# Triangular inverses of a hybrid encoder: from 32x32 elimination on two engines to 16x16 elimination with TensorE products

## The chip, the cores and the metric

The kernel runs on one core of a Trainium2 chip. A core has a matrix engine (TensorE, PE in the profile, with its weight loads as PEld), VectorE (DVE), ScalarE (ACT), GpSimd (POOL), and a queue of DMA transfers that SyncE (SP) issues. Each engine works through its own list of instructions in order and waits for the others by semaphores. The metric is the device time in microseconds from start to end of one execution; it is measured several times, and the median is given.

## What is computed

A bidirectional encoder of two layers on 512 tokens and 1024 features. Each layer normalises its input, projects it once, and splits the columns among three mixers: windowed attention, a gated DeltaNet and an RWKV-7 mixer, the last two in both directions. Their outputs are joined, projected and added to the residual; then comes a gated feed-forward block. The part that matters here is this, from the DeltaNet:

```python
def gated_delta_chunked(q, k, v, g, beta):        # C = 64 tokens per chunk
    ...
    decay = jnp.exp(jnp.where(tril, gc[..., :, None] - gc[..., None, :], -jnp.inf))
    k_beta = k * beta[..., None]
    lower = jnp.where(strict, jnp.einsum('bhnid,bhnjd->bhnij', k_beta, k) * decay, 0.0)
    a_mat = lower + jnp.eye(C, dtype=lower.dtype)
    rhs = jnp.concatenate([v * beta[..., None], k_beta * jnp.exp(gc)[..., None]], -1)
    sol = lax.linalg.triangular_solve(a_mat, rhs, left_side=True, lower=True, unit_diagonal=True)
    ...

def rwkv7_scan(r, w, k, v, a, b):
    ...
    def step(state, inp):
        r_t, w_t, k_t, v_t, a_t, b_t = inp
        sa = jnp.einsum('bhvk,bhk->bhv', state, a_t)
        state = (state * w_t[:, :, None, :] + sa[..., None] * b_t[:, :, None, :]
                 + v_t[..., None] * k_t[:, :, None, :])
        return state, jnp.einsum('bhvk,bhk->bhv', state, r_t)
```

The DeltaNet solves one unit triangular 64x64 system per head, chunk and direction (6 heads, 8 chunks, 2 directions, per layer). The kernel computes RWKV-7 in chunks of 64 too, which gives the same kind of system (4 heads, 8 chunks, 2 directions). The kernel forms the inverse (I-N)^-1 of each of these systems, N strictly triangular, and the scans then multiply by it.

## The kernel before

Activations lie with features on the 128 partitions and the 512 tokens along the row. A projection is 24 matmuls of 128x512 (`product`, L319 to L321: eight k-tiles, each weight and each activation split in two parts). ACT and POOL make the split of the weights (L308, L309) as they arrive.

One layer goes through these stages: RWKV projections; the preparation of RWKV (`rwkv_prep`, for two pairs of heads) in turn with DeltaNet projections and their convolution (`dn_conv`); the RWKV inverses; the RWKV scan of eight steps, with attention projections beside it; `dn_prep`, which forms the DeltaNet matrices; `rwkv_out`; the DeltaNet inverses, with five blocks of attention (`attn_head`) beside them; the DeltaNet scan with the gate projections and more attention; the output projection; the feed-forward block.

A 64x64 matrix lies as `tile[:, chunk, 0:64]`, two heads above each other on the partitions, so a 128-row tile of eight chunks has 32 diagonal 32x32 blocks (four 32-row bands times eight chunks). The inverse of them is made in three steps.

1. Gather. For each band of 32 rows, one ACT copy of 32x256 puts the diagonal blocks of eight chunks into a tile `dpk` of 128 x 32 problems x 32 columns (L511 for RWKV, 16 per layer; L984 for the DeltaNet with the sign turned, 24 per layer; DeltaNet has 24 problems of each direction and 8 empty places).
2. `invert`. DVE transposes `dpk` so that each partition holds whole matrices (L383 or L385), 30 steps of forward elimination follow, each a product and a sum (L390, L391) on r x j columns, r + j = 31, the second waiting for the first; then two transposes (L397, L398) give the inverse as it lies and transposed. RWKV has one such chain, on DVE. The DeltaNet has two, the forward direction on DVE and the backward one on POOL, written in turn, with one block of attention after every sixth step.
3. `finish_inverse` fills in the 32x32 block off the diagonal of each 64x64 matrix by two small products per matrix (L411, a copy by ACT at L413, L417, a copy by ACT at L421) and ACT copies the diagonal blocks into place (L425, again a band of 32x256 at a time).

An attention block goes through PE (scores, L842), DVE (row maximum, L843), ACT (exponential, L852), DVE (L853 to L856), PE (transpose, L859), ACT (copy, L861), PE (L863).

The order on each engine is fixed when the kernel is built: a scheduler places instructions by priority as their inputs come, and tiles of a pool are handed out in the program's order, so a tile's new writer waits for the last reader of the old one. PSUM tiles have four pools: two for projections, three for RWKV and attention projections, two for the DeltaNet and attention, one for attention outputs.

The loop that both stages of the change touch is, for the DeltaNet:

```python
fw, bw = invert(dpks[0], True, V, work[:, :256]), invert(dpks[1], False, G, work[:, 256:])
for i in range(31):
    next(bw)
    next(fw)
    if i % 6 == 5:
        next(att, None)
inv = [run(fw), run(bw)]
```

## Time and profile before

| | |
|---|---|
| median of three runs | 1736.58 us (1732.81 to 1736.79) |
| span of the profiled execution, first to last instruction | 1732.2 us |
| PE busy | 1537.9 us, 89% |
| DVE, ACT, POOL busy | 952.5, 821.4, 704.9 us |
| mean granted clock of PE | 0.929 |

For the profiled execution only its span is known; the 4.4 us between the median and that span are taken as what lies around the span. The page gives totals by engine, and the groups of instructions by line. A table of stretches gives each engine's busy time between two points of the span, with the granted clock of PE as a share of full speed. A timeline gives single instructions, with the idle time ahead of each in brackets and the instruction whose end released it. Line numbers are those of the kernel before.

### The profile page before, as it was taken

To read this page: it belongs to the slowest core of one execution; us is meant where nothing else is said; L and a number is where in the kernel's file an instruction comes from. 1 tells how busy PE (TensorE), PEld (TensorE's weight loads), DVE (VectorE), ACT (ScalarE), POOL (GpSimd) and SP (SyncE) were. 2 spreads that over 40 slices of the span, in tenths; PEclk is the share of its full clock that TensorE was granted. 3 is DMA by queue.
4 is the path that set the end of the run, shared out by engine and by line. 5 is a ranking of instruction groups with operands and counts; after the bars stand their busy time and mean duration, and the time that the engine had idled before them with its cause. 6 is when DMAs were issued, how large, how long until landed. Compare 5 with 4: busy or idle time off the path is not lost. (4 is left out here: it accounts for less than half of the span.)

```text
span 1732.2 us, 29160 instructions
## 1 busy us (share of the span) xinstructions
PE 1537.9 (89%) x11500; PEld 1204.0 (70%) x11500; DVE 952.5 (55%) x1583; ACT 821.4 (47%) x1541; POOL 704.9 (41%) x632
## 2 busy tenths in 40 slices
PE   7988789359999999999998897982799999999997
PEld 4676666247678888888876676651577788888885
DVE  6478945775535555531136797578563455555001
ACT  5556453446445444443335754362744544444321
POOL 4321323431165555545543122426013655555553
PEclk9989979658999999999999998995799999999998
DMA  5311211100043333333342012220002333333332
GB/s 166 79 39 50 63 48 44 37 1 15 26 128 92 97 97 98 97 104 113 114 104 74 20 50 50 59 66 1 2 21 80 110 98 98 97 97 97 93 99 91
DMA packets 230537, 126.07 MB, mean 73 GB/s; under 512 B 23656, under 2 KB 221416, under 8 KB 230400
## 3 DMA queue, kind: packets, MB, share of 16 engines
q1 hardware_dynamic: 228624, 121.02, 25.0%
q10 hardware_dynamic: 1776, 3.20, 0.6%
q8 instruction: 90, 1.47, 0.4%
q14 instruction: 47, 0.39, 0.1%
HBM read 117.84 MB, written 6.34 MB: 72 GB/s over the span
## 5 line engine op out<-in xcount | busy, mean ns | idle before, releaser
L309 POOL TENSOR_TENSOR wl<-wr,wh 128x512 fp32r<-128x512 f32 (+1 forms) x408 | 555.9, 1365 | 760.9 <-ACT wh L308 714.5
L319 PE MATMUL ps<-hh,wh 128*128 128x512 f32 x1248 | 502.7, 403 | 21.2 <-ACT wh L308 18.6
L320 PE MATMUL ps<-hl,wh 128*128 128x512 f32 x1248 | 502.1, 402 | 0.0
L321 PE MATMUL ps<-hh,wl 128*128 128x512 f32 x1248 | 498.7, 400 | 0.4 <-POOL wl L309 0.4
L308 ACT ACTIVATE wh<-wr 128x512 fp32r<-128x512 f32 (+1 forms) x408 | 250.8, 618 | 444.5 <-PE ps L320 393.4
L319 PEld LDWEIGHTS ps<-hh,wh 128*128 128x128 f32 x1248 | 236.4, 190 | 80.2 <-ACT wh L308 19.5
L320 PEld LDWEIGHTS ps<-hl,wh 128*128 128x128 f32 x1248 | 236.3, 189 | 55.8 <-issue 3.7
L321 PEld LDWEIGHTS ps<-hh,wl 128*128 128x128 f32 x1248 | 235.8, 189 | 55.6 <-issue 3.9
L1063 DVE TENSOR_TENSOR p<-ps,p 128x512 f32<-128x512 f32 x16 | 11.1, 692 | 198.8 <-PE ps L321 198.8
L859 PE MATMUL ps<-cst,cv 128*128 128x128 f32 x120 | 24.9, 341 | 85.0 <-DVE cv L856 84.5
L320 PE MATMUL ps<-p,wh 128*128 128x512 f32 x256 | 99.6, 389 | 0.0
L319 PE MATMUL ps<-p,wh 128*128 128x512 f32 x256 | 99.6, 389 | 0.0
L321 PE MATMUL ps<-p,wl 128*128 128x512 f32 x256 | 99.6, 389 | 0.0
L1040 DVE TENSOR_TENSOR tr<-ps,rb 128x512 f32<-128x512 f32 x44 | 30.4, 692 | 100.3 <-PE ps L321 100.3
L859 PEld LDWEIGHTS ps<-cst,cv 128*128 128x128 f32 x120 | 15.7, 168 | 95.5 <-issue 67.4
L747 POOL TENSOR_TENSOR sm<-sm,gl 128x384 f32<-128x384 f32 x12 | 10.8, 903 | 129.9 <-DVE sm L776 72.8
L1043 DVE SCALAR_TENSOR_TENSOR td<-tr,par,td 128x511 f32<-128x511 f32 x44 | 39.1, 889 | 34.9 <-ACT td L1042 34.9
L1043 DVE SCALAR_TENSOR_TENSOR tr<-td,par,tr 128x511 f32<-128x511 f32 x44 | 36.5, 830 | 35.0 <-ACT tr L1042 35.0
L319 PEld LDWEIGHTS ps<-p,wh 128*128 128x128 f32 x256 | 48.1, 188 | 10.0
L321 PEld LDWEIGHTS ps<-p,wl 128*128 128x128 f32 x256 | 48.1, 188 | 9.9
L320 PEld LDWEIGHTS ps<-p,wh 128*128 128x128 f32 x256 | 48.1, 188 | 9.9
L279 POOL TENSOR_TENSOR tr<-tr,tr 128x512 f32<-128x512 f32 x32 | 42.8, 1337 | 28.0 <-issue 8.7
(292 smaller groups left out, 2597.6 us busy)
## 6 DMA issues: line engine op xcount, KB each, us to landing
wr<-ffn_w_up SPq DMA_DIRECT2D x176, 256.0 KB, 2.9
wr<-w_in SPq DMA_DIRECT2D x88, 256.0 KB, 2.8
wr<-ffn_w_down SPq DMA_DIRECT2D x80, 256.0 KB, 2.8
wr<-w_in SPq DMA_DIRECT2D x24, 128.0 KB, 2.4
p<-scr ACTq DMA_DIRECT2D x12, 256.0 KB, 3.6
wr<-w_out SPq DMA_DIRECT2D x32, 96.0 KB, 2.6
wr<-w_out SPq DMA_DIRECT2D x16, 192.0 KB, 3.0
p<-xt SPq DMA_DIRECT2D x8, 256.0 KB, 3.7
```

The source lines that it names most:

```text
L279: G.tensor_tensor(acc, self.acc, sq, add)
L308: S.activation(hi[:, :n, :], raw[:, :n, :], AF.Copy)
L309: G.tensor_tensor(lo[:, :n, :], raw[:, :n, :], hi[:, :n, :].bitcast(F32), sub)
L319: PE.matmul(o, wh, xh, start=k == 0, stop=False)
L320: PE.matmul(o, wh, xl, start=False, stop=False)
L321: PE.matmul(o, wl, xh, start=False, stop=k == n - 1)
L747: G.tensor_tensor(gs, state, flat(gl, step), mult)
L859: PE.transpose(pp[:, P * j : P * j + P], scs[g][:, P * j : P * j + P], ident)
L1040: V.tensor_tensor(u, o, nf.rb, mult)
L1043: V.scalar_tensor_tensor(a[:, 1:], u[:, :-1], w(0), a[:, 1:], mult, add)
L1063: V.tensor_tensor(x1[j], o, x1[j], add)
```

## The change

The elimination works on 16x16 blocks, and what the 32x32 inverse has beside them comes from products on PE. Both DeltaNet directions go through one chain of DVE instructions; POOL no longer eliminates. The ACT gathers by bands become one DVE instruction on all 128 rows with a mask (`diag32`: the left half times a 0/1 column plus the right half, of which the wrong parts are zero). In `invert`:

- L406 gathers the 16x16 diagonal halves of a `dpk` (128x512, masked), L411 transposes them (half as many columns as before); ACT keeps the part off the diagonal in `dpk` (L413), POOL clears the rest (L414).
- 14 steps of elimination, L421 and L422, on X x r x j columns with r + j = 15; X is 2 for RWKV and 4 for the DeltaNet (two halves, two directions).
- Per set of problems two transposes (L430, L431), three masked ACT copies (L434 to L436), and three groups of products with tiles of 32x32 and 16 columns, one product per problem and band: L440, an ACT copy (L442), L445, a DVE sum (L446), L449, a DVE sum (L450). A group has 128 products for RWKV and 96 for each DeltaNet direction.

In `finish_inverse` (L466 and L472 are the products that were L411 and L417) the copies of the diagonal blocks become one masked copy of 128 rows and two copies of 32 rows for eight chunks, where there were four of 32 rows. The DeltaNet loop has 16 turns with one block of attention after every third, five in all as before.

```diff
+    for name, half in (("m16", 16), ("m32", 32)):
+        first = (i // half % 2 == 0).astype(np.float32)
+        add(name, np.stack([first, 1 - first, -first, first - 1], 1))
...
-    def invert(dpk, upper, E, work):
-        L = p4(32, 32)
-        if upper:
-            V.transpose(L, dpk.rearrange("q p t -> q t p"))
-        else:
-            V.transpose(L.rearrange("p s t -> p t s"), dpk.rearrange("q p t -> q t p"))
-        yield
-        for j in range(1, 31):
-            r = 31 - j
-            tmp = work[:, : r * j].rearrange("p (r j) -> p r j", j=j)
-            E.tensor_tensor(tmp, L[:, j + 1 : 32, j : j + 1].broadcast_to([P, r, j]), L[:, j : j + 1, 0:j].broadcast_to([P, r, j]), mult)
-            E.tensor_tensor(L[:, j + 1 : 32, 0:j], L[:, j + 1 : 32, 0:j], tmp, add)
+    def diag32(dst, mt, upper):
+        lo, hi = mt[:, :, 0:32], mt[:, :, 32:64]
+        m = C("m32")
+        if upper:
+            V.scalar_tensor_tensor(dst, hi, m[:, 1:2], lo, mult, add)
         else:
+            V.scalar_tensor_tensor(dst, lo, m[:, 0:1], hi, mult, add)
+
+    def invert(st, dpks, uppers, sign, work, np_):
+        n = len(dpks)
+        m = C("m16")
+        s0 = 0 if sign > 0 else 2
+        L = p4(1024)
+        dc, o1c, o2c = p4(2, 32, 16), p4(2, 32, 16), p4(2, 32, 16)
+        halves = [(slice(0, 16), slice(16, 32)), (slice(16, 32), slice(0, 16))]
+        views = []
+        for x, (dpk, upper) in enumerate(zip(dpks, uppers)):
+            k = 1 if upper else 0
+            first, second = halves[0 if upper else 1]
+            V.scalar_tensor_tensor(dc[:, x], dpk[:, :, second], m[:, s0 + k : s0 + k + 1], dpk[:, :, first], mult, add if sign > 0 else sub)
...
+            V.transpose(byt, dc[:, x].rearrange("q p t -> q t p"))
+            S.activation(dpk[:, :, second], dpk[:, :, second], AF.Copy, scale=m[:, s0 + 1 - k : s0 + 2 - k])
+            G.memset(dpk[:, :, first], 0.0)
             yield
+        X = 2 * n
+        Lv = L[:, : 256 * X].rearrange("p (x r c) -> p x r c", r=16, c=16)
+        for j in range(1, 15):
+            r = 15 - j
+            tmp = work[:, : X * r * j].rearrange("p (x r j) -> p x r j", x=X, j=j)
+            V.tensor_tensor(tmp, Lv[:, :, j + 1 : 16, j : j + 1].broadcast_to([P, X, r, j]), Lv[:, :, j : j + 1, 0:j].broadcast_to([P, X, r, j]), mult)
+            V.tensor_tensor(Lv[:, :, j + 1 : 16, 0:j], Lv[:, :, j + 1 : 16, 0:j], tmp, add)
+            yield
...
+            V.transpose(o1c[:, x].rearrange("q p c -> q c p"), byt)
+            V.transpose(o2c[:, x].rearrange("q p c -> q c p"), bys)
+            o1, o2 = p4(32, 32), p4(32, 32)
+            u = slice(0, np_)
+            S.activation(o1[:, u, first], o1c[:, x, u], AF.Copy, scale=m[:, 1 - k : 2 - k])
+            S.activation(o1[:, u, second], o1c[:, x, u], AF.Copy, scale=m[:, k : k + 1])
+            S.activation(o2[:, u, second], o2c[:, x, u], AF.Copy, scale=m[:, k : k + 1])
+            pw = ps(st, (P, 32, 16))
+            blocks = [(p, slice(h, h + 32)) for p in range(np_) for h in range(0, P, 32)]
+            for p, hs in blocks:
+                PE.matmul(pw[hs, p, :], dpk[hs, p, :], o2c[hs, x, p, :], start=True, stop=True)
+            G.memset(dpk[:, :, second], 0.0)
+            S.activation(dpk[:, u, first], pw[:, u], AF.Copy)
+            px2 = ps(st, (P, 32, 16))
+            for p, hs in blocks:
+                PE.matmul(px2[hs, p, :], o1[hs, p, :], dpk[hs, p, first], start=True, stop=True)
+            V.scalar_tensor_tensor(o2[:, u, first], o2c[:, x, u], m[:, 1 - k : 2 - k], px2[:, u], mult, add)
+            px1 = ps(st, (P, 32, 16))
+            for p, hs in blocks:
+                PE.matmul(px1[hs, p, :], dpk[hs, p, :], o1c[hs, x, p, :], start=True, stop=True)
+            V.tensor_tensor(o1[:, u, second], px1[:, u], o1[:, u, second], add)
...
             for i in range(0, len(grp), 8):
-                mt = grp[i][1]
+                p, mt, _ = grp[i]
+                S.activation(mt[:, :, ra : ra + 32], o1[:, p : p + 8, :], AF.Copy, scale=m[:, ra // 32 : ra // 32 + 1])
                 for h in (0, 64):
+                    S.activation(mt[h + rb : h + rb + 32, :, rb : rb + 32], o1[h + rb : h + rb + 32, p : p + 8, :], AF.Copy)
...
-        for i in range(0, n, 8):
-            p, mt, _ = units[i]
-            for h in range(0, P, 32):
-                S.activation(mt[h : h + 32, :, h % 64 : h % 64 + 32], o1[h : h + 32, p : p + 8, :], AF.Copy)
...
-            for h in range(0, P, 32):
-                S.activation(st["dpk"][h : h + 32, 8 * u : 8 * u + 8, :], gb[h : h + 32, :, h % 64 : h % 64 + 32], AF.Copy)
+            diag32(st["dpk"][:, 8 * u : 8 * u + 8, :], gb[:, :, 0:64], True)
...
-        o1, o2 = run(invert(rw["dpk"], True, V, t2("r")))
+        ((o1, o2),) = run(invert("r", [rw["dpk"]], [True], 1.0, t2("r"), 32))
...
-        work = cv()
-        fw, bw = invert(dpks[0], True, V, work[:, :256]), invert(dpks[1], False, G, work[:, 256:])
-        for i in range(31):
+        bw = invert("d", dpks, [True, False], -1.0, cv(), 8 * NPAIR_DN)
+        for i in range(16):
             next(bw)
-            next(fw)
-            if i % 6 == 5:
+            if i % 3 == 2:
                 next(att, None)
-        inv = [run(fw), run(bw)]
+        inv = run(bw)
```

The scheduler then places the instructions anew. Lines L319 to L321 of before are L323 to L325 of the changed kernel, and the attention lines L842 to L863 are L895 to L916. In the rows below a name is a tile with its number: `ps` a PSUM tile, `p` one of the 20 tiles of four KB per partition, `hh`/`hl` and `wh`/`wl` the parts of activations and weights.

PE before, layer 0, where the RWKV inverse's first product stands: behind the last of a projection's 24 matmuls.

```order
L319 MATMUL ps_2258<-hh_147,wh_2267 128x512
L320 MATMUL ps_2258<-hl_148,wh_2267 128x512
L321 MATMUL ps_2258<-hh_147,wl_2268 128x512
L411 MATMUL ps_1629<-p_1626,p_631 32x32 x16
L411 MATMUL ps_1629<-p_1626,p_656 32x32 x16
L417 MATMUL ps_1665<-p_1625,tr_1630 32x32
L411 MATMUL ps_1702<-p_1626,p_1171 32x32 x16
L411 MATMUL ps_1702<-p_1626,p_1196 32x32 x5
L417 MATMUL ps_1665<-p_1625,tr_1630 32x32 x31
```

PE now, at the same stage: the products of the inverse stand inside a projection (`ps_2353`), and `L746` is a product of `dn_prep` that sums the squares of q or k (L693 before).

```order
L746 MATMUL ps_2218<-td_2216,cst 128x512
L323 MATMUL ps_2353<-hh_117,wh_2356 128x512
L324 MATMUL ps_2353<-hl_118,wh_2356 128x512
L325 MATMUL ps_2353<-hh_117,wl_2357 128x512
L323 MATMUL ps_2353<-hh_126,wh_2362 128x512
L440 MATMUL ps_1594<-p_1553,p_556 32x16 x128
L746 MATMUL ps_2224<-td_2222,cst 128x512
L445 MATMUL ps_1725<-p_556,p_1589 32x16 x128
L449 MATMUL ps_1855<-p_1552,p_556 32x16 x128
L466 MATMUL ps_1985<-p_1590,p_631 32x32 x16
```

Of that projection 14 matmuls stand ahead of L440. What follows the first L466 are the small products of `dn_prep` (L774 and L775); the rest of the projection and the whole next one have moved behind the inverse, among the products of the scan.

DVE before, end of the DeltaNet elimination of layer 0 (`den`, `nmx`, `es` belong to attention): block 4 ends, then the transposes with block 5 between them.

```order
L856 TENSOR_SCALAR cv_3127<-cv_3127,den_3141 128x256
L856 TENSOR_SCALAR cv_3128<-cv_3128,den_3141 128x256
L397 STREAM_TRANSPOSE p_3228<-p_2919 128x32x32
L843 ISA cv_3188,mx_3190<-ps_3191,cst,sink_86 128x256
L843 ISA mx_3190 128x1
L843 ISA cv_3189,mx_3190<-ps_3194,cst,sink_86 128x256
L843 ISA mx_3190 128x1
L398 STREAM_TRANSPOSE p_3229<-p_2919 128x32x32
L847 TENSOR_TENSOR es_3198<-sink_86,mx_3190 128x2
L848 TENSOR_SCALAR nmx_3197<-mx_3190 128x2
L397 STREAM_TRANSPOSE p_3233<-p_2917 128x32x32
L398 STREAM_TRANSPOSE p_3234<-p_2917 128x32x32
```

DVE now, at the same place: the end of block 4, then the transposes with block 5.

```order
L909 TENSOR_SCALAR cv_3397<-cv_3397,den_3411 128x256
L909 TENSOR_SCALAR cv_3398<-cv_3398,den_3411 128x256
L430 STREAM_TRANSPOSE p_3253<-p_3251 128x16x32
L896 ISA cv_3440,mx_3442<-ps_3443,cst,sink_86 128x256
L896 ISA mx_3442 128x1
L896 ISA cv_3441,mx_3442<-ps_3446,cst,sink_86 128x256
L896 ISA mx_3442 128x1
L431 STREAM_TRANSPOSE p_3254<-p_3251 128x16x32
L900 TENSOR_TENSOR es_3450<-sink_86,mx_3442 128x2
L901 TENSOR_SCALAR nmx_3449<-mx_3442 128x2
L430 STREAM_TRANSPOSE p_3253<-p_3251 128x16x32
L431 STREAM_TRANSPOSE p_3254<-p_3251 128x16x32
```

Before, blocks 1 to 3 stood among the steps of the elimination and block 4 between them and L397. Now blocks 1 and 2 stand among the steps, and all of blocks 3 and 4 between the last step and L430.

PE before, from the first scores of attention block 5 to the finish of the DeltaNet inverses.

```order
L842 MATMUL ps_3191<-at_2194,at_2502 128x256
L842 MATMUL ps_3194<-at_2194,at_2502 128x256
L411 MATMUL ps_3237<-p_3229,p_1891 32x32 x16
L411 MATMUL ps_3237<-p_3229,p_2701 32x32 x16
L417 MATMUL ps_3273<-p_3228,td_3238 32x32 x32
L411 MATMUL ps_3310<-p_3229,p_2790 32x32 x16
```

PE now, in the same stage; 96 products of L440 for the forward direction (`p_3480` is one of its results, `p_3240` its matrices) stand ahead of these rows.

```order
L916 MATMUL ps_3439<-tr_3463,at_2654 64x128 x2
L912 MATMUL ps_3468<-cst,cv_3441 128x128 x2
L445 MATMUL ps_3584<-p_3240,p_3480 32x16 x19
L916 MATMUL ps_3439<-tr_3471,at_2654 64x128 x2
L445 MATMUL ps_3584<-p_3240,p_3480 32x16 x77
L449 MATMUL ps_3682<-p_3253,p_3240 32x16 x96
L440 MATMUL ps_3787<-p_3254,p_3245 32x16 x96
L895 MATMUL ps_4448<-at_2546,at_2854 128x384
L445 MATMUL ps_3886<-p_3245,p_3782 32x16 x96
L449 MATMUL ps_3984<-p_3253,p_3245 32x16 x96
L895 MATMUL ps_4451<-at_2546,at_2854 128x384
L466 MATMUL ps_4082<-p_3481,p_2243 32x32 x16
```

Six groups of 96 products now stand between the scores of block 5 and the first product of the finish, which is L466.

## Rows read from the trace of the kernel before

**Rows 1.** The page, engine totals: busy us, share of the span, instructions.

```profile
PE 1537.9 (89%) x11500; PEld 1204.0 (70%) x11500; DVE 952.5 (55%) x1583; ACT 821.4 (47%) x1541; POOL 704.9 (41%) x632
```

**Rows 2.** Groups by line and shape: out<-in xcount | busy us, mean ns | idle before.

```profile
L308 ACT ACTIVATE wh<-wr 128x512 fp32r<-128x512 f32 x388 | 243.2, 630 | 412.3 <-PE ps L320 364.2 <-issue 21.9 <-POOL sm L585 6.9
...
L425 ACT ACTIVATE p<-p 32x256 f32<-32x256 f32 x80 | 33.1, 414 | 15.0 <-DVE p L397 13.8
...
L984 ACT ACTIVATE p<-p 32x256 f32<-32x256 f32 x48 | 19.9, 414 | 0.6
...
L511 ACT ACTIVATE p<-p 32x256 f32<-32x256 f32 x32 | 13.2, 414 | 24.7 <-DVE p L551 24.4
```

**Rows 3.** Busy time by stretch: window, its length, engines (xcount), PEclk, DMA, GB/s.

```profile
181.00:211.00 30.00, 26.43 (x158) 20.26 (x156) 29.42 (x52) 14.37 (x24) 9.25 (x7) 0.94 0.28 63
211.00:228.00 17.00, 6.53 (x203) 5.77 (x201) 8.95 (x15) 7.11 (x16) 1.81 (x3) 0.57 0.20 44
228.00:240.00 12.00, 12.00 (x108) 7.94 (x110) 0.43 (x2) 7.27 (x18) 2.54 (x2) 0.50 0.18 45
240.00:312.00 72.00, 71.37 (x849) 50.02 (x845) 49.53 (x85) 30.34 (x60) 26.92 (x32) 1.00 0.23 63
312.00:336.00 24.00, 0.61 (x5) 0.40 (x4) 15.65 (x32) 14.55 (x38) 8.25 (x18) 0.58 0.05 13
336.00:378.00 42.00, 19.65 (x76) 11.63 (x75) 37.04 (x90) 10.96 (x31) 24.79 (x46) 0.54 0.00 1
378.00:398.00 20.00, 17.99 (x412) 13.66 (x414) 6.99 (x17) 16.18 (x42) 0.00 (x0) 0.67 0.01 2
```

**Rows 4.** Timeline of DVE, RWKV inverse: start us, us, operation, [idle before <-releaser].

```profile
160.99 0.73 DVE L649 SCALAR_TENSOR_TENSOR cv<-td,par,cv 128x510 f32<-128x510 f32 x1
...
165.40 1.98 DVE L383 STREAM_TRANSPOSE p<-p 128x1024 f32<-128x1024 f32 x1
...
169.35 0.25 DVE L390 TENSOR_TENSOR tr<-p 128x84 f32<-128x84 f32 x1
...
215.53 1.91 DVE L397 STREAM_TRANSPOSE p<-p 128x1024 f32<-128x1024 f32 x1
217.30 1.97 DVE L398 STREAM_TRANSPOSE p<-p 128x1024 f32<-128x1024 f32 x1
```

**Rows 5.** Timeline of PE, same stage.

```profile
185.32 1.39 PE L693 MATMUL ps<-td,cst 128*128 128x512 f32 x2 [3.57 <-ACT td L691]
...
219.32 1.91 PE L411 MATMUL ps<-p,p 32*32 32x32 f32 x64 [8.01 <-DVE p L398]
...
227.06 0.31 PE L417 MATMUL ps<-p,tr 32*32 32x32 f32 x2 [1.78 <-ACT tr L413]
```

**Rows 6.** Timeline of DVE, DeltaNet inverses of layer 0.

```profile
316.92 0.69 DVE L635 TENSOR_TENSOR p<-p,tr 128x512 f32<-128x512 f32 x1
325.72 1.97 DVE L385 STREAM_TRANSPOSE p<-p 128x1024 f32<-128x1024 f32 x1 [8.11 <-ACT p L984]
...
337.13 0.64 DVE L390 TENSOR_TENSOR cv<-p 128x168 f32<-128x168 f32 x1
...
362.79 0.33 DVE L390 TENSOR_TENSOR cv<-p 128x168 f32<-128x168 f32 x1
...
367.81 0.48 DVE L843 CUSTOM_DVE_ANT_0 cv<-ps,cst,sink 128x256 f32<-128x256 f32 x1 [0.21 <-PE ps L842]
...
375.19 0.48 DVE L843 CUSTOM_DVE_ANT_0 cv<-ps,cst,sink 128x256 f32<-128x256 f32 x1 [1.84 <-PE ps L842]
...
376.00 2.01 DVE L398 STREAM_TRANSPOSE p<-p 128x1024 f32<-128x1024 f32 x1
```

**Rows 7.** Timeline of PE, end of the DeltaNet inverses and first scan product.

```profile
378.15 1.92 PE L411 MATMUL ps<-p,p 32*32 32x32 f32 x64 [3.00 <-DVE nmx L848]
...
389.00 1.20 PE L411 MATMUL ps<-p,p 32*32 32x32 f32 x63
...
397.88 1.54 PE L762 MATMUL ps<-p,p 64*64 64x64 f32 x22
```

More of the change, by code (lines that the diff above doesn't have):

```diff
@@ L375, in run @@
                 return e.value
-    def invert(dpk, upper, E, work):
-        L = p4(32, 32)
+    def diag32(dst, mt, upper):
+        lo, hi = mt[:, :, 0:32], mt[:, :, 32:64]
+        m = C("m32")
         if upper:
-            V.transpose(L, dpk.rearrange("q p t -> q t p"))
+            V.scalar_tensor_tensor(dst, hi, m[:, 1:2], lo, mult, add)
         else:
-            V.transpose(L.rearrange("p s t -> p t s"), dpk.rearrange("q p t -> q t p"))
-        yield
-        for j in range(1, 31):
-            r = 31 - j
-            tmp = work[:, : r * j].rearrange("p (r j) -> p r j", j=j)
-            E.tensor_tensor(tmp, L[:, j + 1 : 32, j : j + 1].broadcast_to([P, r, j]), L[:, j : j + 1, 0:j].broadcast_to([P, r, j]), mult)
-            E.tensor_tensor(L[:, j + 1 : 32, 0:j], L[:, j + 1 : 32, 0:j], tmp, add)
-            yield
-        Lf = L.rearrange("p a b -> p (a b)")
-        G.memset(Lf[:, 0:1024:33], 1.0)
-        o1, o2 = p4(32, 32), p4(32, 32)
-        nat, swp = L, L.rearrange("p a b -> p b a")
-        V.transpose(o1.rearrange("q p c -> q c p"), nat if upper else swp)
-        V.transpose(o2.rearrange("q p c -> q c p"), swp if upper else nat)
-        return o1, o2
+            V.scalar_tensor_tensor(dst, lo, m[:, 0:1], hi, mult, add)
@@ new lines, in invert @@
+    def invert(st, dpks, uppers, sign, work, np_):
[10 more added lines that the diff above has]
+            V.scalar_tensor_tensor(dc[:, x], dpk[:, :, second], m[:, s0 + k : s0 + k + 1], dpk[:, :, first], mult, add if sign > 0 else sub)
+            Lx = L[:, 512 * x : 512 * x + 512]
+            byt = Lx.rearrange("p (b r c) -> p r b c" if upper else "p (b r c) -> p c b r", b=2, r=16)
+            bys = Lx.rearrange("p (b r c) -> p c b r" if upper else "p (b r c) -> p r b c", b=2, r=16)
+            views.append((byt, bys))
+            V.transpose(byt, dc[:, x].rearrange("q p t -> q t p"))
+            S.activation(dpk[:, :, second], dpk[:, :, second], AF.Copy, scale=m[:, s0 + 1 - k : s0 + 2 - k])
+            G.memset(dpk[:, :, first], 0.0)
+            yield
+        X = 2 * n
[6 more added lines that the diff above has]
+            yield
+        G.memset(L[:, : 256 * X].rearrange("p (x y) -> p x y", y=256)[:, :, 0:256:17], 1.0)
+        outs = []
+        for x, (dpk, upper) in enumerate(zip(dpks, uppers)):
+            k = 1 if upper else 0
+            first, second = halves[0 if upper else 1]
+            byt, bys = views[x]
+            V.transpose(o1c[:, x].rearrange("q p c -> q c p"), byt)
[19 more added lines that the diff above has]
+            V.tensor_tensor(o1[:, u, second], px1[:, u], o1[:, u, second], add)
+            outs.append((o1, o2))
+            yield
+        return outs
@@ L404, in finish_inverse @@
         n = len(units)
+        m = C("m32")
         for g0 in range(0, n, 16):
@@ L982, in layer @@
             for p in range(NPAIR_DN):
-                for h in range(0, P, 32):
-                    S.activation(dpk[h : h + 32, 8 * p : 8 * p + 8, :], dn["rm"][p][d][h : h + 32, :, h % 64 : h % 64 + 32], AF.Copy, scale=-1.0)
+                diag32(dpk[:, 8 * p : 8 * p + 8, :], dn["rm"][p][d][:, :, 0:64], d == 0)
             dpks.append(dpk)
-        work = cv()
-        fw, bw = invert(dpks[0], True, V, work[:, :256]), invert(dpks[1], False, G, work[:, 256:])
-        for i in range(31):
+        bw = invert("d", dpks, [True, False], -1.0, cv(), 8 * NPAIR_DN)
+        for i in range(16):
             next(bw)
-            next(fw)
-            if i % 6 == 5:
+            if i % 3 == 2:
                 next(att, None)
-        inv = [run(fw), run(bw)]
+        inv = run(bw)
         for d in range(2):
```

## The prediction

> **What bounds the kernel now.** I read the page's engine totals first: TensorE (PE) is busy for 1537.9 of 1732.2 us [rows 1], so nearly all of the time that another engine can still give back lies where PE waits or runs at a low clock. The table of stretches shows where: around the two kinds of triangular inverse. In the RWKV stage of layer 0, PE loses 3.57 us of 181–211 and 10.47 us of 211–228, and the clock granted is 0.57 there and 0.50 in the 12 us behind it, which is the lower of its two levels; then 72 us run full at 1.00. In the DeltaNet stage PE has work for 0.61 of 24 us and for 19.65 of the next 42, at a clock of 0.54 to 0.58 [rows 3]. The timelines say who is waited for. RWKV: PE's first product of the inverse (L411) stands after 8.01 us of idle until VectorE (DVE) ends L398, the last step of the elimination [rows 4, 5]. DeltaNet: DVE waits 8.11 us for the 24 gathers on ScalarE (ACT) before it may start, then eliminates until about 367.6 between pieces of attention, and PE's L411 starts at 378.15 [rows 6, 7]. So the elimination ends last in both stages, and the rest of the program (projections, feed-forward: PE full) is not touched.
>
> **RWKV, per layer: what goes.** PE's losses that the inverse causes, by [rows 3]: idle 3.57 + 10.47 + 0.63 (of 240–312) = 14.7 us; cold work, busy time times what the clock lacks, 26.43 x 0.06 + 6.53 x 0.43 + 12.00 x 0.50 = 10.4 us. Together 25.1 us, if the elimination ends so early that PE still has projections to do. It does: 60 instructions of 30 to 240 columns become 28 of 28 to 112. An 84-column one takes 0.25 us [rows 4]; with gaps I take 0.26 each, 7.3 us. The order puts 14 convolution steps between them, 0.73 us each [rows 4], 10.2 us. From 167 us, the start before, the end is thus near 185 (188 if some collide with GpSimd, POOL, as 168 columns do at 0.64 against 0.33 in [rows 6]), not 215. The two transposes behind it are half as wide: 1.0 us each by L397 and L398 [rows 4]. So the 3.57 us at 181–185 go as well, since DVE is then no longer late with the convolution for which L693 waits. The 16 ACT gathers of 414 ns [rows 2] become 4 masked DVE steps of about 0.4 us (estimate, between 168 columns at 0.33 and 510 at 0.73), hidden beside projections; if that cover were gone they would cost 1.6 us.
>
> **RWKV: what comes.** 3 x 128 products of 32x32 on 16 columns stand on PE's own queue, so they cost their pitch in full. The trace has no such shape; nearest are the 32-column products of the same tile size: 63 in 1.20 us warm (19 ns) and 64 in 1.92 us cold (30 ns) [rows 7]. Half the columns can't be slower than the cold row unless the arrangement matters (a rival, below), and could be half the warm row: 10 to 31 ns, 3.8 to 11.9 us. I take 19 ns, since PE is warm by then: 7.3 us. *Trainium skill, "TensorE: Matmul & The Clock Gate", section "Wait — 56ns, not 53.3ns?": start to start is never below about 25 ns however few the columns. The 19 ns of [rows 7] are below that, so the row decides here; by the page the sum would be 2.3 us per layer higher.* New waits inside the tail: L440 on L431 about 2.5 us, a filler product on its ACT source 1.3, ACT's copy of the first product (a 128x512 copy is 0.63, [rows 2]) 0.3 beyond its filler, and the copies in finish_inverse that queue on ACT 3.3: 7.4 us, all estimates from the order with these durations; bounds 4 and 10. Work that falls cold in these waits: 3 us (0 to 6, against 10.4 now). Projection matmuls that stood ahead of the inverse are moved into the scan behind it, where the same 72 full microseconds take them at the same price. The memsets on POOL wait only for L406 and L411, so the weight splits queued behind them are not held up. Sum: 25.1 - 7.3 - 7.4 - 3 = 7.4; I take **7 us gained per layer**. Ends: 25.1 - 3.8 - 4 = 17 and 25.1 - 11.9 - 10 - 6 = -3.
>
> **DeltaNet, per layer, as a clock time of layer 0.** Start: the last DVE step ahead ends at 317.6 [rows 6]. Before, DVE idles 8.11 for the gathers (24 of 414 ns on ACT, [rows 2]), and two transposes of up to 1.97 follow: 329.6. Now four masked steps (1.6), two L406 (0.73 each, as 510 columns in [rows 4]), two half transposes (2.0): 322.7. Elimination: both directions in 28 DVE instructions of 56 to 224 columns; 168 columns take 0.33 alone and 0.64 beside POOL's own elimination [rows 6], which is gone, so 0.22 to 0.39 each, with gaps 10 us. Two attention blocks stand between them (2.3 us of DVE each) with 1.4 of waits: 338.7. What is late next: attention. The order now puts blocks 3 and 4 wholly ahead of L430, and only block 5 between the transposes. A block costs DVE, ACT and PE in turn: 367.81 to 375.19, 7.4 us [rows 6]; of 384 columns I take 8.2. So 355.1. L430 hides in the chain to block 5's first step (before: a transpose of 1.91, [rows 4], and 1.84 idle, [rows 6], so 3.7), then that step (0.9) and L431 (1.0): 360.7, where L398 began at 376.00 before. So some 17 us are won by here.
>
> Then a tail that did not exist: 6 x 96 products, cold and with little beside them. At 22 ns (between the 19 and the 30 of [rows 7], for four tiles in turn where the row has two) 12.7 us; bounds 15 and 31, 8.6 to 17.9. Between them stand hops through ACT and DVE, a wait for block 5's exponentials, and two scratch tiles that the second direction gets only after the first's L449: about 7 us (5 to 9). L466 comes at 380.5, 2.3 us later than L411 at 378.15 before. The finish took 19.7 us to L762 [rows 7], paced by ACT's copies (414 ns, [rows 2]); of six copies per eight blocks one goes, so 2.5 us less, and 0.8 less for the longer overlap: 396.9 against 397.88, and 1 more since the finish's first copies no longer queue behind seven L425. **2 us gained per layer**, between -4 and +7.
>
> **Sum.** 2 x (7 + 2) = 18 us off the profiled span of 1732.2: 1714. The median of the runs, 1736.58, is 4.4 above that span, taken as what lies around it and unchanged: **1718 us**.
>
> **Rivals.**
> - *The tail is cheap* (warm, below 19 ns, with waits covered): RWKV 12, DeltaNet 6 per layer, 36 us: 1700. For it: the 25.1 us that PE loses are all there to be had. Against: the order shows no wide filler between L440 and L466.
> - *The tail eats it*: all 1920 products at the cold row's 31 ns and the upper bounds of the waits. RWKV 25.1 - 11.9 - 8 - 4 = +1, DeltaNet -2 to 0 : about 1737. For it: [rows 3] show how readily the clock falls to 0.50 to 0.58 here. Against: projections stand just ahead in RWKV.
> - *Slower: products that take turns.* The new products go round four row groups and write one accumulator bank. If those exclude each other, a product occupies its tile alone. The 30 ns of [rows 7] with two tiles in turn are then 60 for one, cold, and 38 warm: 384 x (38 - 19) + 576 x (60 - 22) = 29 us more per layer, 1718 + 58 = 1776. It decides from about 31 ns per product (18 us over 1920 products are 9 ns). Against: L411 already alternates two row groups into one bank and reaches 19 ns [rows 7]. *Trainium skill, "TensorEngine Tiling (Array Packing)", section "Gotcha 1: PSUM Pressure": different row tiles cannot access the same PSUM bank at the same time, a rule against this change; L411's row doesn't show such a price for two row groups, and no run here shows four.*
> - *It doesn't do what it says in DeltaNet*: if attention blocks, not the elimination, set the end, the stage stays as it is, and only RWKV's 14 us count: 1722, inside the forecast's own range.
>
> **How the numbers follow.** Forecast 1718, own range 1708 to 1728: 0.52, the last rival in it. Cheap tail, below 1708: 0.18. Tail eats it, 1728 to 1742: 0.16. Slower beyond: 0.14. About 0.3%, 5.2 us, is what a measurement of this kernel can tell from no change, so faster means below 1731.4 and slower above 1741.8. Of the third case 0.04 lies below 1731.4 and 0.12 between: faster 0.74, same 0.12, slower 0.14. For 8 in 10 the range leaves out the slower case and a little of the cheap one: 1700 to 1738.
>
> **What would show it.** Right: DVE's elimination ends near 185 in RWKV; the idle of 8.01 before the inverse's first product is below 3; the 12 cold us after it shrink; in DeltaNet the first elimination is near 323, L431 near 361, and L440, L445 and L449 take about 2 us per 96. Wrong: a pitch of the 16-column products above 31 ns; L466 later than 383; attention blocks that hold L430 beyond 356; or convolutions that are late in RWKV although the elimination is short. If DeltaNet's scan still starts at 398 and RWKV's stage is 7 us shorter, the split of the sum is right but not its second term.

## The result, and the profile after

The changed kernel takes 1777.20 us (median of four runs, 1767.65 to 1783.95) against 1734.82 (1732.81 to 1736.79): a ratio of 1.0241, 95% interval 1.0207 to 1.0275. It is slower by 42 us, where 18 us of gain were forecast. The profiled execution is one of the longer ones: its span is 1782.2 us, 50.0 more than that of [rows 1]. In a run further down, the DeltaNet half alone, one of five executions, the profiled one, took 2546.84 us at a mean granted clock of 0.552: that run's ratio leaves it out, and its profile is not read.

The totals of the page after (columns as in [rows 1]), its row of granted clock over 40 slices, and the queue that carries instructions:

```profile
PE 1620.2 (91%) x15340; PEld 1267.7 (71%) x15340; DVE 927.3 (52%) x1493; ACT 788.5 (44%) x1471; POOL 643.4 (36%) x522
...
PEclk9998599656999999999999986995589999999998
...
q8 instruction: 120, 1.97, 0.4%
```

PE has 3840 matmul records more than in [rows 1], and as many weight loads, although the change adds 1920 products. So each float32 product is two records and two loads. The instruction queue of the kernel before, from its page:

```profile
q8 instruction: 90, 1.47, 0.4%
```

Thirty packets and 0.50 MB more for 7680 instructions more: 256 instructions to a packet, which is 128 matmul records with their loads. The totals agree: twice 11500 and twice 15340 instructions of PE are 89.8 and 119.8 times 256, and the queue moved 90 and 120 packets.

First and last start of the steps that matter, in us, read from the views of their lines (the elimination on DVE, the products L440 to L449, the first product of the finish, and the first and last L575 or L628 and the first L762 or L815 for the scans):

| | before | after |
|---|---|---|
| layer 0, RWKV elimination | 167.4 to 215.0 | 162.9 to 180.6 |
| RWKV products | none | 184.4 to 204.6 |
| finish begins | 219.3 | 204.5 |
| RWKV scan | 227.3 to 286.5 | 216.2 to 294.3 |
| DeltaNet elimination | 329.7 to 367.2 | 330.8 to 344.4 |
| DeltaNet products | none | 367.5 to 398.1 |
| finish begins | 378.2 | 399.8 |
| DeltaNet scan begins | 397.9 | 423.9 |
| layer 1, RWKV scan begins | 1077.3 | 1090.1 |
| DeltaNet elimination begins | 1180.1 | 1204.6 |
| DeltaNet scan begins | 1247.4 | 1297.5 |

The eliminations did what was expected of them. The products behind them last 20 and 31 us. The timeline of PE after shows why, in the second half of the DeltaNet products (against [rows 7]):

```profile
384.09 1.90 PE L440 MATMUL ps<-p,p 32*32 32x16 f32 x128 [1.55 <-issue]
387.54 0.51 PE L440 MATMUL ps<-p,p 32*32 32x16 f32 x22 [1.55 <-issue]
387.99 1.65 PE L895 MATMUL ps<-at,at 64*128 64x384 f32 x2
389.56 2.75 PE L445 MATMUL ps<-p,p 32*32 32x16 f32 x189
...
394.31 1.90 PE L449 MATMUL ps<-p,p 32*32 32x16 f32 x128 [1.41 <-issue]
397.77 0.52 PE L449 MATMUL ps<-p,p 32*32 32x16 f32 x24 [1.55 <-issue]
398.21 1.65 PE L895 MATMUL ps<-at,at 64*128 64x384 f32 x2
399.79 1.92 PE L466 MATMUL ps<-p,p 32*32 32x32 f32 x64
```

128 records run in 1.90 us, 14.8 ns each (13.3 from start to start, since the last record alone lasts 0.2 us; the 19 and 30 ns of [rows 7] are reckoned like the 14.8), then PE stands for 1.4 to 1.6 us, and the releaser is "issue": nothing that the profile shows is waited for. From 384.09 to 387.54 it is 128 records in 3.45 us, 27 ns per record or 54 per product. 128 records are just one packet of instructions. Elsewhere in these products a pause stands 128 or some 256 records behind the one before, which is one packet or two.

The transfers of these packets are in the same profile. The view of the DMA engines from 360 to 400 us, one number per us:

```profile
GB/s 0 0 0 0 0 0 0 0 0 16 0 0 0 0 16 0 0 16 0 0 0 16 0 0 0 16 0 0 16 0 0 0 16 0 0 16 0 0 16 8
q8 instruction: 9, 0.15, 1.5%
```

Each 16 is one packet of the instruction queue. From 374 on one comes every 3 to 4 us, and almost nothing else is moved. Views of 2 us put two of them at 381.7 and 385.2; PE goes on at 384.09 and 387.54, 2.4 us behind each. The DMA engines are busy with them for 1.5% of the time, so it is not their load that sets this pace; what sets it stays open.

The groups of the three products, with the idle time ahead of them:

```profile
L449 PE MATMUL ps<-p,p 32*32 32x16 f32 x1280 | 20.5, 209 | 17.9 <-issue 17.9
L445 PE MATMUL ps<-p,p 32*32 32x16 f32 x1280 | 19.8, 210 | 4.1 <-issue 3.9
L440 PE MATMUL ps<-p,p 32*32 32x16 f32 x1280 | 19.4, 206 | 13.6 <-issue 9.6 <-DVE nmx L901 4.1
```

31.4 us of PE's idle time in the whole kernel stand ahead of these lines with "issue" as the cause. In layer 0 it is 7.0 us in RWKV (184 to 207, first three rows: total us, times, longest) and 8.2 in the DeltaNet (367.5 to 399.8):

```profile
PE ps L449 <- issue: 3.9, 2, 2.4
PE ps L445 <- issue: 1.8, 1, 1.8
PE ps L440 <- issue: 1.3, 1, 1.3
...
PE ps L449 <- issue: 4.8, 3, 1.8
PE ps L440 <- issue: 3.1, 2, 1.6
PE ps L440 <- DVE nmx L901: 2.0, 1, 2.0
PE ps L445 <- issue: 0.3, 1, 0.3
```

Stretches after, which answer to [rows 3] (columns as there; the first three RWKV, the last two DeltaNet):

```profile
184.40:204.50 20.10, 13.12 (x763) 11.16 (x767) 5.57 (x8) 4.39 (x8) 1.75 (x2) 0.50 0.17 43
204.50:216.20 11.70, 11.70 (x288) 10.41 (x280) 0.84 (x3) 8.51 (x19) 0.00 (x0) 0.50 0.02 4
216.20:230.00 13.80, 13.80 (x144) 9.51 (x144) 4.67 (x9) 5.87 (x14) 1.29 (x1) 0.59 0.08 20
367.50:399.80 32.30, 23.92 (x1170) 19.55 (x1170) 5.79 (x13) 9.39 (x23) 1.05 (x2) 0.50 0.02 5
399.80:423.90 24.10, 24.10 (x409) 17.81 (x408) 3.08 (x8) 14.57 (x33) 0.00 (x0) 0.50 0.01 2
```

The clock stands at 0.50 from 184 to 216, where [rows 3] have 0.50 to 0.57 from 211 to 240, and from 367 to 424, the finish included, which ran at 0.67 in [rows 3].

### The profile page after: what moved, and what is told of

It is laid out like the page before. It is cut to its first block, busy times and chain, and to the rows that moved or that the text cites. A ratio compares the mean times of both kernels' runs of the same rounds, so it can differ in the third digit from the quotient of the medians.

```text
span 1782.2 us, 36591 instructions
## 1 busy us (share of the span) xinstructions
PE 1620.2 (91%) x15340; PEld 1267.7 (71%) x15340; DVE 927.3 (52%) x1493; ACT 788.5 (44%) x1471; POOL 643.4 (36%) x522
## 3 DMA queue, kind: packets, MB, share of 16 engines
q1 hardware_dynamic: 228624, 121.02, 24.1%
q10 hardware_dynamic: 1776, 3.20, 0.6%
## 5 line engine op out<-in xcount | busy, mean ns | idle before, releaser
L323 PE MATMUL ps<-hh,wh 128*128 128x512 f32 x1248 | 506.0, 406 | 18.4 <-ACT wh L312 18.2
L325 PE MATMUL ps<-hh,wl 128*128 128x512 f32 x1248 | 505.4, 405 | 0.4 <-POOL wl L313 0.4
L323 PEld LDWEIGHTS ps<-hh,wh 128*128 128x128 f32 x1248 | 237.5, 191 | 78.7 <-ACT wh L312 19.0
L325 PEld LDWEIGHTS ps<-hh,wl 128*128 128x128 f32 x1248 | 237.7, 190 | 57.8 <-issue 3.9
L323 PE MATMUL ps<-p,wh 128*128 128x512 f32 x256 | 99.6, 389 | 0.0
L325 PE MATMUL ps<-p,wl 128*128 128x512 f32 x256 | 99.6, 389 | 0.0
L1093 DVE SCALAR_TENSOR_TENSOR td<-tr,par,td 128x511 f32<-128x511 f32 x44 | 49.5, 1124 | 39.2 <-ACT td L1092 39.2
L1098 DVE TENSOR_TENSOR tr<-tr,td 128x512 f32<-128x512 f32 x44 | 57.7, 1311 | 1.5
L1094 DVE SCALAR_TENSOR_TENSOR tr<-td,par,tr 128x511 f32<-128x511 f32 x44 | 57.0, 1296 | 1.6
L325 PEld LDWEIGHTS ps<-p,wl 128*128 128x128 f32 x256 | 48.1, 188 | 10.1
L323 PEld LDWEIGHTS ps<-p,wh 128*128 128x128 f32 x256 | 48.1, 188 | 9.9
```

The lines of the kernel that those rows point to most:

```text
L323: PE.matmul(o, wh, xh, start=k == 0, stop=False)
L325: PE.matmul(o, wl, xh, start=False, stop=k == n - 1)
L1093: V.scalar_tensor_tensor(a[:, 1:], u[:, :-1], w(0), a[:, 1:], mult, add)
L1094: V.scalar_tensor_tensor(a[:, :-1], u[:, 1:], w(2), a[:, :-1], mult, add)
L1098: V.tensor_tensor(acts[0], acts[0], acts[1], mult)
```

## The experiments

The theory from here on is S: in the new products PE is short of instructions. A product costs four of them, a packet of 256 comes about every 3.45 us, and PE uses one up in 1.9 us. The rivals are named in each expectation. Diffs are against the changed kernel unless said otherwise, and are cut to the lines that matter. Every ratio is against the kernel before, run anew beside each experiment (1732.58 to 1735.44 us).

**Halves of the change.** The first run takes the RWKV inverse of the changed kernel and the DeltaNet of before, the second the other way round (shown: the second, where `invert32` is the elimination of before; its gathers and finish are those of before too).

```diff
-        ((o1, o2),) = run(invert("r", [rw["dpk"]], [True], 1.0, t2("r"), 32))
+        o1, o2 = run(invert32(rw["dpk"], True, V, t2("r")))
```

> The change in the RWKV inverse alone (its gathers, elimination, products and finish); the DeltaNet inverses are those of the kernel before. Theory S (PE is short of instructions in the new products: a float32 product is two matmul records, and after about 128 records, each with its weight load, PE idles some 1.55 us with 'issue' as the releaser): the stage costs about 8 us per layer against before, so 16 us in all, about 1751. My prediction's sum had -7 per layer, 1721. Rival P (no shortage, only twice the records at the pitch of 14.6 ns and a cold clock): 768 records are 11.2 us instead of 7.3, so -3 per layer, 1729.

> The change in the DeltaNet inverses alone; RWKV as before. Theory S: 17.7 us per layer more, 35 in all, about 1770, with the six groups of products (L440, L445, L449) lasting 31 to 33 us from the first to L466. Rival P: 1152 records of 14.6 ns are 16.8 us instead of 12.7, so the stage would stay within 3 us of before: 1730 to 1741. If the two halves add up, this and the RWKV half alone give the 42 us of the whole.

Measured: 1755.58 us, ratio 1.0134 (1.0100 to 1.0167), and 1753.85, 1.0116 (1.0086 to 1.0146). Each half alone loses, and 23.0 + 21.3 = 44 us give the 42 of the whole. RWKV costs more than S had (16), the DeltaNet less (35). S took its 17.7 from the profiled execution after, which was 6.8 us longer than the median; that is half of the 14 us at most, and the rest of the difference stays open. In the RWKV half's trace the DeltaNet elimination begins at 339.1, 9.4 us later than before. P is out for both.

**Only the masked gathers.** Against the kernel before; the second run also keeps the old `finish_inverse`. Shown for the DeltaNet; RWKV has the same.

```diff
-                for h in range(0, P, 32):
-                    S.activation(dpk[h : h + 32, 8 * p : 8 * p + 8, :], dn["rm"][p][d][h : h + 32, :, h % 64 : h % 64 + 32], AF.Copy, scale=-1.0)
+                diag32(dpk[:, 8 * p : 8 * p + 8, :], dn["rm"][p][d][:, :, 0:64], d == 0, True)
```

> Only the masked gathers and the masked copies of the finish; elimination of 32x32 blocks on DVE and POOL as before, no new products. All theories that put the loss on the products: the DeltaNet elimination starts 6 to 7 us earlier (323 instead of 329.7), ACT has less to do in the finish, RWKV unchanged or up to 2 us worse from the DVE steps in a full DVE. About 1722 (1718 to 1728). If the masked steps themselves cost, 1735 or above.

> Only the masked gathers; elimination and finish as before. The masked gathers with the changed finish won 8.8 us up to the first product of the finish in layer 0 and lost 6.3 from there to the scan. If the changed copies of the finish and what the scheduler puts beside them lose it, the scan now starts 7 to 9 us earlier than before in each layer: 1716 to 1722. If the loss is only moved work (a projection that comes ahead of the scan instead of in it), it stays at about 1729.

Measured: 1729.05 us, 0.9983 (0.9963 to 1.0003), and 1723.70, 0.9934 (0.9912 to 0.9957). Both lie just above what was expected (up to 1728 and 1722), and the first can't be told from no change. In the DeltaNet the gathers are worth about what was expected: the elimination begins 37.3 us after the RWKV scan's last L575 (43.2 before), 5.9 us won where 6 to 7 were expected. RWKV, expected to stay or to lose up to 2 us, wins too: its scan begins at 223.8 and 223.2 instead of 227.3, so that the DeltaNet elimination begins at 320.9 and 317.4 instead of 329.7. With the changed finish 26.0 us pass from its first product to the scan, with the old one 22.8 (19.7 in layer 1, as in [rows 7]). The gathers alone beat the kernel before by 0.7%, and the new copies of the finish, with what the scheduler puts beside them, give over half of it back.

**Attention behind the inversion.**

```diff
-            if i % 3 == 2:
+            if i in (2, 5):
                 next(att, None)
         inv = run(bw)
+        for i in range(3):
+            next(att, None)
```

> The changed kernel with attention blocks 3 to 5 written behind the DeltaNet inversion, so that the transposes and the products follow the elimination at once and attention runs beside the products. Theory S: the products' 31 us are set by instructions and not by PE or by the wait for attention, so they start some 16 us earlier, and attention's instructions (about a hundred) cost them 1 to 3 us: first product of the finish near 384 instead of 399.8, 1777 - 2 x 15 = about 1747. Rival O (the order is the loss; attention and products each need PE in turn): the attention blocks only change places with the products, 1770 to 1780.

Measured: 1750.99 us, 1.0101 (1.0073 to 1.0129), 26 us less than the changed kernel. The timeline of PE in this run:

```profile
348.98 0.52 PE L440 MATMUL ps<-p,p 32*32 32x16 f32 x24 [0.64 <-DVE p L431]
...
360.11 1.90 PE L449 MATMUL ps<-p,p 32*32 32x16 f32 x128 [1.55 <-issue]
363.84 0.66 PE L449 MATMUL ps<-p,p 32*32 32x16 f32 x34 [1.82 <-issue]
...
381.97 0.84 PE L466 MATMUL ps<-p,p 32*32 32x32 f32 x22
```

The products start 18.5 us earlier and again last 33 us to the first product of the finish, with the same pauses of 1.55 and 1.82 us, although three blocks of attention now lie among them and behind. The order was a loss of its own, and the length of the products did not depend on it. O, by which attention and products would only have changed places (1770 to 1780), falls.

**One record per product.** The operands are the upper halves of the float32 words, so the lower 16 bits are left out of these products; nothing else changes.

```diff
-                PE.matmul(pw[hs, p, :], dpk[hs, p, :], o2c[hs, x, p, :], start=True, stop=True)
+                PE.matmul(pw[hs, p, :], dpk.bitcast(BF16)[hs, p, 1::2], o2c.bitcast(BF16)[hs, x, p, 1::2], start=True, stop=True)
```

> The changed kernel with the operands of the new products read as the upper 16 bits of each float32 word, so that a product is one weight load and one matmul instead of two of each (the lower bits of these operands are left out). Theory S (supply of instructions, 128 matmul records per 3.45 us): the products of RWKV take 10 us instead of 20.2, those of the DeltaNet 15 to 17 instead of 30.6; with less cold time behind them about 1725 (1715 to 1735). Rival W (the time lies in the waits between the groups: copies on ACT, sums on DVE, two scratch tiles): they stay above 17 and 25, 1755 or more.

Measured: 1718.96 us, 0.9913 (0.9878 to 0.9948). The products take 9.3 and 5.5 us in RWKV (layers 0 and 1) instead of 20.2 and 20.8 (the 5.5 at a granted clock of 0.99), and 15.7 and 17.3 in the DeltaNet instead of 30.6 and 30.3. PE in the RWKV products:

```profile
184.56 1.19 PE L441 MATMUL ps<-p,p 32*32 32x16 bf16 x128
185.72 1.10 PE L747 MATMUL ps<-td,cst 128*128 128x512 f32 x2
186.75 0.87 PE L446 MATMUL ps<-p,p 32*32 32x16 bf16 x92
189.08 0.43 PE L446 MATMUL ps<-p,p 32*32 32x16 bf16 x36 [1.46 <-issue]
189.34 0.96 PE L450 MATMUL ps<-p,p 32*32 32x16 bf16 x92
193.63 0.43 PE L450 MATMUL ps<-p,p 32*32 32x16 bf16 x36 [3.33 <-issue]
```

Between the two pauses lie 36 + 92 = 128 records again. They run faster and the pause is longer (3.33 us), so the packet still sets the time; here 4.55 us pass from one resumption to the next, not 3.45, while weights come in by DMA (share 0.24). W falls: the copies on ACT and the sums on DVE are the same as before.

**Work in the pauses.** A needless product of 128x128x128 after every 16 products of the DeltaNet, in all three groups.

```diff
+                if np_ < 32 and n_ % 16 == 15:
+                    PE.matmul(pw[:, 24:32, :], ident, ident, start=True, stop=True)
```

> The changed kernel with a needless float32 product of 128x128x128 into an unused part of the accumulator after every 16 products of the DeltaNet (36 per layer, 72 records of about 0.25 us at the low clock, 18 us of work, and 144 more instructions to some 2300). Theory S: PE does it while it would wait for instructions, so the products last 30.6 + 2 to 4 us, and the whole 2 to 10 us more, about 1783; if the clock rises it may even be less. Rival P (PE is busy with the products, the gaps are drains of PE that any product pays): 18 us more per layer, 48 us for the products, 1813.

Measured: 1828.95 us, 1.0543 (1.0464 to 1.0622), two executions, above what S and P had. Timeline and stretches of this run:

```profile
383.00 0.62 PE L447 MATMUL ps<-p,p 32*32 32x16 f32 x32
383.56 0.80 PE L449 MATMUL ps<-cst 128*128 128x128 f32 x2
384.28 0.62 PE L447 MATMUL ps<-p,p 32*32 32x16 f32 x32
384.84 0.80 PE L449 MATMUL ps<-cst 128*128 128x128 f32 x2
```

```profile
364.80:418.90 54.10, 54.10 (x1245) 41.00 (x1245) 7.84 (x21) 10.97 (x28) 1.05 (x2) 0.50 0.01 3
418.90:443.20 24.30, 24.30 (x412) 17.95 (x411) 2.20 (x4) 14.86 (x33) 0.00 (x0) 0.50 0.01 2
```

The size of the filler was wrong: the pair takes 0.72 us from start to start, 26 us per layer and not 18. But the pauses are gone. 34 records now take 1.28 us, 38 ns each and slower than the 27 ns at which instructions come, and PE is busy for 54.1 of 54.1 us where it stood 8.2 us for "issue" after. So 26 us of work cost 54.1 - 32.3 = 22 us although the products' own pitch rose to 17.5 ns from start to start; the rest filled pauses. The two layers make 44 of the 52 us by which this run is longer than the changed kernel; where the other 8 lie was not looked at. P (each product pays a drain) would have kept them.

**Twice the columns, the same instructions** (`c2` is 2 for the DeltaNet and 1 for RWKV; so in all three groups).

```diff
-                PE.matmul(pw[hs, p, :], dpk[hs, p, :], o2c[hs, x, p, :], start=True, stop=True)
+                PE.matmul(pw[hs, p : p + c2, :], dpk[hs, p, :], o2c[hs, x, p : p + c2, :], start=True, stop=True)
```

> The changed kernel with 32 instead of 16 columns in each DeltaNet product (the second 16 fall on the next problem's place and are overwritten by its own product), the same number of instructions. Theory S: the columns cost up to 30 ns per record at the low clock (64 records of 32 columns took 1.92 us), 34 us for 1152, instead of 27 ns of supply: the products last 33 to 37 us instead of 30.6, 1783 to 1790. Rival P (a record's time is its columns plus a fixed loss): 30.6 + 17 = 47 us, 1810.

Measured: 1779.33 us, 1.0257 (1.0206 to 1.0308), two executions, as the changed kernel; the products last 34.9 and 33.7 us. Timeline and stretches:

```profile
383.41 1.93 PE L441 MATMUL ps<-p,p 32*32 32x32 f32 x128 [2.07 <-issue]
387.41 0.54 PE L441 MATMUL ps<-p,p 32*32 32x32 f32 x24 [2.07 <-issue]
387.88 1.65 PE L896 MATMUL ps<-at,at 64*128 64x384 f32 x2
389.46 2.84 PE L446 MATMUL ps<-p,p 32*32 32x32 f32 x192
```

```profile
363.70:400.20 36.50, 25.01 (x1174) 20.12 (x1174) 7.63 (x21) 10.72 (x28) 1.05 (x2) 0.55 0.02 4
400.20:418.90 18.70, 18.38 (x409) 13.83 (x408) 2.19 (x4) 14.65 (x33) 0.00 (x0) 0.74 0.01 3
```

128 records of 32 columns take 1.93 us, as many as with 16. Columns cost nothing here, the count of instructions does. P is out again. S's 33 to 37 us were met, but by luck: it had up to 30 ns of columns per record, and the record took 15; what made the products longer are pauses of 2.07 us, which stay unexplained.

**Fewer instructions in full float32.** L449 forms the transpose of what L445 forms, so one DVE transpose can stand for it. The first run does so with late attention (the memset of `dpk` ahead of the second group goes too); the second also gives RWKV its 32x32 elimination back, and both stages the old finish.

```diff
-            px1 = ps(st, (P, 32, 16))
-            for p, hs in blocks:
-                PE.matmul(px1[hs, p, :], dpk[hs, p, :], o1c[hs, x, p, :], start=True, stop=True)
-            V.tensor_tensor(o1[:, u, second], px1[:, u], o1[:, u, second], add)
+            V.transpose(o1[:, u, :], o2[:, u, :])
```

> The changed kernel with attention blocks 3 to 5 behind the inversion, and the third group of products (L449, its sum and a memset) replaced by one DVE transpose of the result, in full float32: a third of the new instructions goes. Theory S (what PE can be fed): the products of RWKV last about 13 instead of 20.2 us, those of the DeltaNet about 21 instead of 31, and one transpose of 1.5 to 2 us each comes: 7 and 8 us per layer off the 1751 of the late attention, about 1721 (1712 to 1732). Rival H (what made the run with 16-bit operands fast is the narrower operands): the products keep their pitch, the gain is the third of PE's busy time alone, 4 and 6 us per layer less 2 for the transpose and its wait: about 1738.

> RWKV with masked gathers and 32x32 elimination as in the run of the gathers with the old finish; DeltaNet by 16x16 blocks with late attention and the transpose instead of the third group, in full float32. If RWKV's half of the change is still a loss, this is faster than the run with both: by the 11 us per layer that RWKV alone lost, less the 7 that the transpose gives back, 8 us in all: about 1713. If RWKV's half has become a gain it is 5 to 10 us slower.

Measured: 1720.42 us, 0.9913 (0.9882 to 0.9945), and 1710.65, 0.9858 (0.9832 to 0.9885). The products last 15.3 and 16.2 us in RWKV and 19.8 and 20.7 in the DeltaNet. Their pitch and pauses are the old ones, in the first of the two runs:

```profile
347.69 1.90 PE L440 MATMUL ps<-p,p 32*32 32x16 f32 x128 [1.71 <-issue]
351.41 0.66 PE L440 MATMUL ps<-p,p 32*32 32x16 f32 x33 [1.83 <-issue]
```

S's two numbers, 1721 and 1713, came within 3 us, the second partly by luck: its expectation counted only RWKV. In the two profiled executions, 16 us apart, 7 us are won up to the ends of the RWKV scans, and 9 us from there to the DeltaNet scans, where the old finish is the difference. H falls: the number of instructions was the lever, not the width of the operands. The mixed kernel computes in full float32 and beats both kernels by 1.4% and 3.7%.

**Both cures at once.** One record per product, as above, and attention blocks 3 to 5 behind the inversion.

> Both cures of the DeltaNet stage together: one record per product as in the run with 16-bit operands (the lower 16 bits of these operands are left out), and attention blocks 3 to 5 behind the inversion. Theory S: the late attention won 26 us where the products took 30.6 us; with products of 15 to 17 us they end before the attention blocks beside them, so the win is the 3 x 8 us of attention less the products' own 16, 8 to 16 us per layer: 1719 - 16 to 32 = about 1695. If the two cures remove the same loss (the wait of the products for their turn), it stays at 1715 to 1720.

Measured: 1687.60 us, 0.9727 (0.9701 to 0.9754), 31 us below the run with one record alone. The order of attention and the number of instructions were two losses, and they add up: 58 us and 26 us alone, 90 together, against the changed kernel.

## Why the prediction was wrong, point by point

- **What bounds the kernel**: right. PE waited for the elimination in both stages; shortened, it was no longer waited for in RWKV, and in the DeltaNet L431 ended 1.6 us earlier than forecast.
- **Eliminations**: right within 5 us. RWKV's ended at 181 (forecast 185). The DeltaNet's began 4.9 us after the last step ahead of it (5.1), L431 of the first direction ended 41.5 us after that step (43.1). The DVE rows of after:

```profile
330.77 0.24 DVE L421 TENSOR_TENSOR cv<-p 128x56 f32<-128x56 f32 x1
...
344.67 0.22 DVE L422 TENSOR_TENSOR p<-p,cv 128x56 f32<-128x56 f32 x1
...
361.76 1.04 DVE L430 STREAM_TRANSPOSE p<-p 128x512 f32<-128x512 f32 x1
...
366.34 1.05 DVE L431 STREAM_TRANSPOSE p<-p 128x512 f32<-128x512 f32 x1
```

- **The count behind "19 ns" and "22 ns" per product**: the step that failed first. "63 in 1.20 us" in [rows 7] was taken as 63 products. The order of before has two rows of x16 for one group of L411, 32 products, and the trace has x64 for it in [rows 5] and [rows 7]: two records each. The count was off by two. Per record PE was faster than in those rows, 14.8 ns at the low clock, so a product keeps it busy for 29.6 ns, where 22 were taken for the DeltaNet (576 x 7.6 = 4.4 us more) and 19 for RWKV (384 x 10.6 = 4.1 us more).
- **The products on "PE's own queue, so they cost their pitch in full"**: the step that failed most. The sum had no term for instructions that PE has not yet got. Waiting for them cost 8.2 us in the DeltaNet tail and 7.0 in RWKV's of layer 0. With the 4.4 above that is 12.6 us, and the tail from L431 to L466 took 32.4 instead of 19.8. The 7 us that this tail had besides the products were met in size, but by attention's work on PE (about 6.5 us in the timeline) and not by the hops through ACT and DVE. So two signs of being wrong came: 54 ns per product between two pauses (sign: 31), and L466 at 399.8 (sign: 383). [Rows 5 to 7] could not show it: L411 comes 64 records at a time, half a packet, and at 30 ns each it is slower than the 27 ns at which instructions come. *The Trainium skill, "Runtime: NRT & Kernel Launch", section "Instruction fetch mechanics", says that instructions come in blocks of 256 and that fetching is hidden since engines issue more slowly than it fills. The blocks agree with this trace (30 packets for 7680 instructions, pauses 128 or some 256 records apart), the hiding does not (1.4 to 1.8 us of idle at five of the six pauses of the DeltaNet).*
- **RWKV's sum**: idle did fall, from 22.8 us (140 to 317.6) to 18.0 (140 to 326, up to the same step). But cold work rose from 14.9 to 23.3 us, where 10.4 had been written down to 3. With some 5 us for the 768 records that is +8, not -7. "PE is warm by then" was the wrong choice: the clock is 0.50 from 184 to 216. Nor did the 3.57 us ahead of L693 go: PE still stands 3.39 us ahead of L746, its counterpart (`180.66 2.08 PE L746 MATMUL ps<-td,cst 128*128 128x512 f32 x2 [3.39 <-ACT td L744]`). And the 7.4 us of waits inside the tail are luck: 7.0 were measured, but PE waited there for nothing but instructions, and for none of the copies and transposes on the list.
- **The finish**: forecast 16.4 us, measured 24.1. Between its first product and the scan the order has 24 matmuls of a projection where before it had 10, and all ran at 0.50. In the run with 32 columns the same list took 18.7 us at 0.74, so some 5 us of it are the clock. With the tail's 12.6 and 1.6 us won ahead of it, these 7.7 make the 18.7 us by which the DeltaNet of layer 0 took longer than forecast, from its last step ahead to the scan.
- **The rivals**: "products that take turns" gave 1776 us, and 1777 was measured, but for another reason. It had 60 ns per product by tiles that exclude each other; at most 54 were paid, nearly half of them waiting for instructions. Four row groups writing one bank ran at 14.8 ns per record where the two of [rows 7] take 30, and twice the columns changed nothing. So four row groups in one bank show no price here. The rival's chance of 0.14 held the outcome, its mechanism did not: that the number came out is luck.

## What to carry to other kernels

The small matmuls of this kernel were paid by instructions, not by columns: count four for each float32 product (two loads, two matmuls), compare a row of the order with the count in the trace, and compare the pitch with the 27 ns per load and matmul at which this PE was fed. A long run of small products faster than that waited here, and nothing in its data or semaphores showed for it but "issue"; the view of the DMA engines has the packets. Fewer instructions (a transpose instead of a third group, one record instead of two) were the cure. Larger work fills the pauses, but pays only if it has to be done anyway. Work that only waits in turn, such as attention here, belongs behind the start of such a run and not ahead of it.

## What the runs showed of the hardware that was not expected

- PE was fed with 256 instructions about every 3.4 us at best in these stretches, and its pauses reached 3.33 us where weights were loaded by DMA beside it (DMA share 0.17 to 0.24 in RWKV, 0.02 in the DeltaNet). Whether the loads lengthen the pauses was not tried.
- The granted clock stayed at 0.50 through 54.1 us in which PE was busy without a gap, and through 24.3 us more behind it, in the run with filler. In the run with 32 columns it was 0.55 and then 0.74, although PE had stood for 11.5 us in between. So pauses are not what held it down; what did was not settled.
- With four row groups in turn a record takes 14.8 ns at the lower clock level, with 16 columns and with 32 alike; with two, and 32 columns, 30 ns.
